# Residual layer norm: the DRAM rows of a partition in blocks of 24, 24 and 16 instead of 64, with 27 transfers in place of 24

## The chip, the cores and the metric

One core of one Trainium2 chip. The time is device microseconds (us) of one execution, the median of several. A comparison is given as a ratio with a 95% interval: the mean time of one kernel's fast runs over that of the other's of the same rounds on the same chip, so it is not quite the ratio of the medians that are quoted beside it.

## The reference

```
z = x + residual                      # x, residual: 16 x 1024 x 512, float32
mean, var = z.mean(-1), z.var(-1)
out = gamma * (z - mean) / sqrt(var + eps) + beta
```

16,384 rows of 512 elements: 33.55 MB each of x, residual and out.

## The kernel before

There are 128 rows for each of the 128 partitions. GpSimd (POOL) adds x and residual, ScalarE (ACT) takes mean, sum of squares and root, VectorE (DVE) normalises, in turns of 4 rows. x and the result share a ring of 64 rows (zbuf), the residual and the sum a ring of 32 (rbuf). All large transfers go through the sync engine's queue in the order of a plan; `x0+16` is a load of rows 0 to 15 of x, `r` of the residual, `o` a store.

```
BLOCK = 64
PLAN = """
x0+16 r0+8 r8+24 x16+20 x36+28 r32+16 o0+16 o16+8
r48+16 x64+24 r64+16 o24+24 r80+16 x88+16 r96+12 o48+16
x104+8 r108+8 x112+16 r116+12 o64+16 o80+24 o104+16 o120+8
"""
    def dram(t, lo, n):                # which DRAM rows are row lo.. of each partition
        b0 = lo - lo % BLOCK
        v = t[P * b0 : P * (b0 + BLOCK), :].rearrange("(p j) d -> p j d", p=P)
        return v[:, lo - b0 : lo - b0 + n, :].rearrange("p a b -> p (a b)")
... (cut)
    for kind, lo, n in moves:          # the sync engine, in the order of the plan
        if kind == "x":                # the ring's old rows must be stored
            while gone < len(stores) and stores[gone][0] < lo + n - Z_ROWS:
                nc.sync.wait_ge(so[gone], 16)
                gone += 1
            move(part(zbuf, Z_ROWS, lo, n), dram(xf, lo, n), sx[...])
        elif kind == "r":              # the ring's old rows must be used up by DVE
            ... (cut)
        else:                          # the rows must be finished
            ... (cut)
```

With a block of 64, the 64 rows of a partition lie together in DRAM, and the next partition starts 64 x 2 KB = 128 KB further on. This distance is called the pitch below. Each transfer becomes one packet per partition, so 8 for each of the 16 DMA engines (the 3456 packets of the queue are 24 x (128 + 16); the 16 are of 4 bytes).

Of the kernel before, what the change touches and what calls it, by code (L numbers as in the profile page):

```python
# [8 lines left out]
FP32 = mybir.dt.float32  # L9
# [1 line left out]
ALU = mybir.AluOpType  # L11


BLOCK = 64
Z_ROWS = 64
R_ROWS = 32


PLAN = """
x0+16 r0+8 r8+24 x16+20 x36+28 r32+16 o0+16 o16+8  # L20
r48+16 x64+24 r64+16 o24+24 r80+16 x88+16 r96+12 o48+16
x104+8 r108+8 x112+16 r116+12 o64+16 o80+24 o104+16 o120+8
"""


ADDS = [4] * 32


TURN = 4
R_TURNS = R_ROWS // TURN  # L30
Z_TURNS = Z_ROWS // TURN


EARLY = 2
# [3 lines left out]
def kernel(  # L38
# [9 lines left out]
    nc = tc.nc  # L48
    P = nc.NUM_PARTITIONS
# [3 lines left out]
    N, D = xf.shape  # L53
    inv_d = 1.0 / float(D)
    total = N // P


    tc.close()
    tc.compile()  # L59
# [1 line left out]
    moves = []  # L61
    for word in PLAN.split():
        kind, (lo, n) = word[0], map(int, word[1:].split("+"))
        assert lo // BLOCK == (lo + n - 1) // BLOCK
        moves.append((kind, lo, n))

    def of_kind(kind):
# [3 lines left out]

    def dram(t, lo, n):

        b0 = lo - lo % BLOCK
        v = t[P * b0 : P * (b0 + BLOCK), :].rearrange("(p j) d -> p j d", p=P)
        return v[:, lo - b0 : lo - b0 + n, :].rearrange("p a b -> p (a b)")

    zbuf = nc.alloc_sbuf_tensor("zbuf", [P, Z_ROWS * D], FP32)
# [4 lines left out]
    nm, ssq, std, rstd = (  # L83
        nc.alloc_sbuf_tensor(name, [P, R_ROWS], FP32) for name in ("nm", "ssq", "std", "rstd")
    )
    gamma_p = nc.alloc_psum_tensor("gamma_p", [P, D], FP32)
    beta_p = nc.alloc_psum_tensor("beta_p", [P, D], FP32)
    junk_m = [nc.alloc_psum_tensor(f"junk_m{i}", [P, D], FP32) for i in range(TURN)]
    junk_s = [nc.alloc_psum_tensor(f"junk_s{i}", [P, D], FP32) for i in range(6 - TURN)]
    junk_s += [  # L90
        nc.alloc_sbuf_tensor(f"junk_s{i}", [P, D], FP32) for i in range(6 - TURN, TURN)
    ]

    sems = []
# [1 line left out]
    def sem(name):  # L96
        s = nc.alloc_semaphore(name)
        sems.append(s)
        return s
# [5 lines left out]
    s_const = sem("const")  # L105
    s_pe = sem("pe")
    s_sum, s_mean, s_ssq, s_std = (
        [sem(f"{name}{j}") for j in range(R_TURNS)] for name in ("sum", "mean", "ssq", "std")
    )
    s_rstd = [sem(f"rstd{j}") for j in range(Z_TURNS)]  # L110
    s_out = sem("out")
    so = [sem(f"so{c}") for c in range(len(stores))]
    nums = [s.num for s in sems]
# [2 lines left out]
    def part(buf, size, lo, n):  # L116
        assert lo % size + n <= size
        return buf[:, (lo % size) * D : (lo % size + n) * D]
# [16 lines left out]
    seen = 0  # L135
    first = []

    def move(out, in_, s):
        i = nc.sync.dma_start(out=out, in_=in_).then_inc(s, 16)  # L139
        if len(first) < EARLY:  # L140
            first.append(i.ins)

    gone = 0
    for kind, lo, n in moves:
        if kind == "x":
# [3 lines that stand above are left out]
            move(part(zbuf, Z_ROWS, lo, n), dram(xf, lo, n), sx[loads_x.index((lo, n))])  # L149
        elif kind == "r":  # L150
            if lo + n > R_ROWS:
                last = (lo + n - R_ROWS) // TURN - 1
                nc.sync.wait_ge(s_rstd[last % Z_TURNS], last // Z_TURNS + 1)
            move(part(rbuf, R_ROWS, lo, n), dram(rf, lo, n), sr[loads_r.index((lo, n))])
        else:
            if lo + n > seen:
                nc.sync.wait_ge(s_out, lo + n)
                seen = lo + n
            move(dram(of, lo, n), part(zbuf, Z_ROWS, lo, n), so[stores.index((lo, n))])


# [5 lines left out]


    landed = {"x": 0, "r": 0}
    lo = 0  # L170
    for n in ADDS:
        for key, loads, s in (("x", loads_x, sx), ("r", loads_r, sr)):
            while landed[key] < len(loads) and loads[landed[key]][0] < lo + n:
                nc.gpsimd.wait_ge(s[landed[key]], 16)
                landed[key] += 1
        z = part(rbuf, R_ROWS, lo, n)
        nc.gpsimd.tensor_tensor(  # L177
            out=z, in0=part(zbuf, Z_ROWS, lo, n), in1=z, op=ALU.add
        ).then_inc(s_sum[lo // TURN % R_TURNS], 1)
        lo += n  # L180
    assert lo == total



# [1 line left out]
    def column(t, lo, n=1):  # L186
        return t[:, lo % R_ROWS : lo % R_ROWS + n]
# [5 lines left out]
    with act.Fori(0, total // R_ROWS) as lap:  # L193
        hints.append(act.mark_branch_hint_location())
        due = act.snap(lap + 1)
        for j in range(R_TURNS):
            rows = range(j * TURN, (j + 1) * TURN)
            act.wait_ge(s_sum[j], due)
            for k, r in enumerate(rows):
                i = act.activation(  # L200
                    out=junk_m[k][:, :],
                    in_=part(rbuf, R_ROWS, r, 1),
                    func=ACT.Identity,
                    scale=-inv_d,
                    accum_out=column(nm, r),
                )
            i.then_inc(s_mean[j], 1)
            act.wait_ge(s_mean[j], due)
            for k, r in enumerate(rows):
                i = act.activation(  # L210
                    out=junk_s[k][:, :],
                    in_=part(rbuf, R_ROWS, r, 1),
                    func=ACT.Square,
                    bias=column(nm, r),
                    accum_out=column(ssq, r),
                )
            i.then_inc(s_ssq[j], 1)
            act.wait_ge(s_ssq[j], due)
            act.activation(  # L219
                out=column(std, rows[0], TURN),  # L220
                in_=column(ssq, rows[0], TURN),
                func=ACT.Sqrt,
                bias=eps_t[:, 0:1],
                scale=inv_d,
            ).then_inc(s_std[j], 1)


    dve = nc.vector
    dve.wait_ge(s_pe, 2)
    with dve.Fori(0, total // Z_ROWS) as lap:  # L230
        hints.append(dve.mark_branch_hint_location())
        due = [dve.snap(lap * 2 + 1), dve.snap(lap * 2 + 2)]
        turn = dve.snap(lap + 1)
        for j in range(Z_TURNS):
            rows = range(j * TURN, (j + 1) * TURN)
            dve.wait_ge(s_std[j % R_TURNS], due[j // R_TURNS])
            for r in rows:
                dve.scalar_tensor_tensor(  # L238
                    out=part(zbuf, Z_ROWS, r, 1),
                    in0=part(rbuf, R_ROWS, r, 1),  # L240
                    scalar=column(nm, r),
                    in1=gamma_p[:, :],
                    op0=ALU.add,
                    op1=ALU.mult,
                )
            dve.reciprocal(  # L246
                out=column(rstd, rows[0], TURN), in_=column(std, rows[0], TURN)
            ).then_inc(s_rstd[j], 1)
            dve.wait_ge(s_rstd[j], turn)
            for r in rows:  # L250
                z = part(zbuf, Z_ROWS, r, 1)
                i = dve.scalar_tensor_tensor(  # L252
                    out=z,
                    in0=z,
                    scalar=column(rstd, r),
                    in1=beta_p[:, :],
                    op0=ALU.mult,
                    op1=ALU.add,
                )
            i.then_inc(s_out, TURN)  # L260


    loops = [b for b in nc.main_func.blocks if b.name.endswith("_loop")]
# [48 lines left out]
```

## Time and profile before

| | before |
|---|---|
| time, median | 238.22 us at first; 238.04 with all 6 runs beside the changed kernel |
| span of the profile | 236.9 us |
| the data queue's share of 16 engines | 99.3% |
| busiest compute engine | ACT, 78% |
| bytes moved | 100.67 MB |

The page, the stretches and the sync engine's waits are shown and read in the prediction. One thing that the prediction lacks can be had from the packet records: a transfer ends on each engine with a packet of 4 bytes (384 of them for the 24 transfers, 9 ns each), so sorting these in groups of 16 tells when each engine was done with it. (The records don't name the engine; the groups rest on the order in time.) A "round" is one packet on each of the 16 engines.

```
kernel before          first engine   mean    last engine   last - mean
end of x0+16              11.27       11.54      11.76          0.23
end of r32+16             70.37       70.57      70.92          0.35
end of the last store    235.31      235.81     236.43          0.62
```

### The profile page before, as it was taken

The page shows a single profiled execution, that of the slowest core. Times are in us where ns is not written, and L with a number is a line of the kernel's source. Part 1 is how long each engine was busy: PE and PEld are TensorE (multiplying, and loading weights), DVE is VectorE, ACT ScalarE, POOL GpSimd, SP SyncE. Part 2 cuts the span into 40 slices and gives each one's busy share as a digit, 9 for nine tenths or more (in the row PEclk, how much of TensorE's full clock was granted, in tenths as well). Part 3 has the DMA queues.
Part 4 walks back from the last instruction along what each step waited for, and adds up shares of the span by engine and source line. Part 5 has one row for each costly group of instructions (what it writes and reads, how often), then busy time and mean ns, then how long its engine had stood idle before and what let it go on. Part 6 is the DMA issues. An engine that isn't in the chain of part 4 may idle for free.

```text
span 236.9 us, 985 instructions
## 1 busy us (share of the span) xinstructions
PE 4.1 (2%) x4; PEld 1.0 (0%) x4; DVE 177.2 (75%) x290; ACT 184.1 (78%) x545; POOL 144.1 (61%) x36
## 2 busy tenths in 40 slices
PE   0600000000000000000000000000000000000000
PEld 0100000000000000000000000000000000000000
DVE  0000395898999299979997999889999999979900
ACT  2003968999992999799989999899999999799100
POOL 0019468699409990899179936999939375970000
DMA  9999999979999999999999899999999999999997
GB/s 354 399 443 473 456 408 415 508 329 465 443 354 443 393 465 423 490 398 398 443 407 506 382 426 431 422 431 441 409 423 451 425 436 429 479 407 431 437 396 329
DMA packets 3461, 100.67 MB, mean 425 GB/s; under 512 B 387, under 2 KB 387, under 8 KB 389
## 3 DMA queue, kind: packets, MB, share of 16 engines
q1 hardware_dynamic: 3456, 100.66, 99.3%
q10 hardware_dynamic: 4, 0.00, 0.0%
q14 instruction: 1, 0.00, 0.0%
HBM read 67.11 MB, written 33.55 MB: 425 GB/s over the span
## 4 chain that ended last, share of the span: by engine, by line
DMA 44%; ACT 36%; POOL 8%; DVE 6%; issue 1%; SPq 0%; DVEq 0%
DMA rbuf<-in_residual_dram 26%; ACT junk_s L210 19%; DMA zbuf<-in_x_dram 17%; ACT junk_m L200 16%; POOL rbuf L177 8%; DVE zbuf L238 5%; ACT std L219 2%; DVE zbuf L252 1%; DVE rstd L246 0%; SPq L139 0%; DVEq L230 0%
## 5 line engine op out<-in xcount | busy, mean ns | idle before, releaser
L177 POOL TENSOR_TENSOR rbuf<-zbuf,rbuf 128x2048 f32<-128x2048 f32 x32 | 143.9, 4528 | 67.3 <-DMA rbuf<-in_residual_dram 54.2
L238 DVE SCALAR_TENSOR_TENSOR zbuf<-rbuf,nm,gamma_p 128x512 f32<-128x512 f32 x128 | 87.1, 743 | 45.3 <-ACT std L219 45.3
L200 ACT ACTIVATE junk_m<-rbuf 128x512 f32<-128x512 f32 x128 | 74.3, 581 | 31.1 <-POOL rbuf L177 30.9
L210 ACT ACTIVATE junk_s<-rbuf,nm 128x512 f32<-128x512 f32 x128 | 88.9, 694 | 1.0
L252 DVE SCALAR_TENSOR_TENSOR zbuf<-zbuf,rstd,beta_p 128x512 f32<-128x512 f32 x128 | 87.1, 744 | 1.1
L210 ACT ACTIVATION_READ_ACCUMULATOR junk_s<-rbuf,nm 128x1 f32 x128 | 23.9, 187 | 0.0
L200 ACT ACTIVATION_READ_ACCUMULATOR junk_m<-rbuf 128x1 f32 x128 | 23.9, 186 | 0.0
L219 ACT ACTIVATE std<-ssq,eps_t 128x4 f32<-128x4 f32 x32 | 9.5, 297 | 1.0
L246 DVE RECIPROCAL rstd<-std 128x4 f32<-128x4 f32 x32 | 5.5, 171 | 0.0
L191 ACT ACT_TABLE_LOAD x1 | 1.3, 1283 | 2.7 <-PEq L59 2.7
L130 PE MATMUL gamma_p<-gb_row,ones 1*128 1x512 f32 x2 | 2.0, 1122 | 7.3 <-DMA gb_row<-in_gamma_dram 7.3
L130 PE MATMUL beta_p<-gb_row,ones 1*128 1x512 f32 x2 | 2.1, 1136 | 0.4 <-DMA gb_row<-in_beta_dram 0.4
L125 DVE MEMSET ones<- 1x128 f32 x1 | 0.2, 165 | 2.0 <-PEq L59 2.0
L130 PEld LDWEIGHTS gamma_p<-gb_row,ones 1*128 1x128 f32 x2 | 0.5, 308 | 7.3 <-issue 7.3
L130 PEld LDWEIGHTS beta_p<-gb_row,ones 1*128 1x128 f32 x2 | 0.5, 304 | 2.0 <-DMA gb_row<-in_beta_dram 2.0
L293 POOL MEMSET const-float32-0.0<- 128x1 f32 x1 | 0.1, 98 | 0.2 <-issue 0.2
L293 POOL MEMSET const-bfloat16-1.0<- 128x1 bf16 x1 | 0.1, 101 | 0.0
L293 POOL MEMSET const-uint8-127<- 128x1 uint8 x1 | 0.1, 101 | 0.0
L293 POOL MEMSET const-float32-1.0<- 128x1 f32 x1 | 0.1, 98 | 0.0
L126 DVE MEMSET eps_t<- 128x1 f32 x1 | 0.1, 59 | 0.0
## 6 DMA issues: line engine op xcount, KB each, us to landing
rbuf<-in_residual_dram SPq DMA_DIRECT2D x4, 4096.0 KB, 19.4
out_dram<-zbuf SPq DMA_DIRECT2D x4, 4096.0 KB, 26.8
zbuf<-in_x_dram SPq DMA_DIRECT2D x3, 4096.0 KB, 19.3
out_dram<-zbuf SPq DMA_DIRECT2D x2, 6144.0 KB, 31.5
zbuf<-in_x_dram SPq DMA_DIRECT2D x1, 7168.0 KB, 57.8
rbuf<-in_residual_dram SPq DMA_DIRECT2D x1, 6144.0 KB, 29.6
zbuf<-in_x_dram SPq DMA_DIRECT2D x1, 6144.0 KB, 23.7
rbuf<-in_residual_dram SPq DMA_DIRECT2D x2, 3072.0 KB, 19.8
```

What stands on the lines that cost most here:

```text
L125: nc.vector.memset(ones[:, :], 1.0).then_inc(s_const, 1)
L126: nc.vector.memset(eps_t[:, :], float(eps)).then_inc(s_const, 1)
L130: nc.tensor.matmul(dest[:, :], ones[:, :], gb_row[:, k * D : (k + 1) * D], start=True, stop=True).then_inc(s_pe, 1)
L177: nc.gpsimd.tensor_tensor(out=z, in0=part(zbuf, Z_ROWS, lo, n), in1=z, op=ALU.add).then_inc(s_sum[lo // TURN % R_TURNS], 1)
L191: act.preload_act_table_set("sqrt_and_others")
L200: i = act.activation(out=junk_m[k][:, :], in_=part(rbuf, R_ROWS, r, 1), func=ACT.Identity, scale=-inv_d, accum_out=column(nm, r),)
L210: i = act.activation(out=junk_s[k][:, :], in_=part(rbuf, R_ROWS, r, 1), func=ACT.Square, bias=column(nm, r), accum_out=column(ssq, r),)
L219: act.activation(out=column(std, rows[0], TURN), in_=column(ssq, rows[0], TURN), func=ACT.Sqrt, bias=eps_t[:, 0:1], scale=inv_d,).then_inc ...
L238: dve.scalar_tensor_tensor(out=part(zbuf, Z_ROWS, r, 1), in0=part(rbuf, R_ROWS, r, 1), scalar=column(nm, r), in1=gamma_p[:, :], op0=ALU.ad ...
L246: dve.reciprocal(out=column(rstd, rows[0], TURN), in_=column(std, rows[0], TURN)).then_inc(s_rstd[j], 1)
L252: i = dve.scalar_tensor_tensor(out=z, in0=z, scalar=column(rstd, r), in1=beta_p[:, :], op0=ALU.mult, op1=ALU.add,)
L293: nc = _bacc.Bacc("TRN2", target_bir_lowering=False, num_devices=1)
```

## The change

Every transfer's rows are to lie in one DRAM block, so a load of 24 rows becomes one contiguous piece of 6 MB, and the pitch falls to 48 KB (32 KB in the blocks of 16). The plan is recut to fit; the opening load grows from 16 to 24 rows and the last store shrinks from 8 to 4. The rest of the diff generalises the arithmetic of rows and turns; the turns stay 32 of 4 rows.

```
-BLOCK = 64
+BLOCKS = [24, 24, 16]
 PLAN = """
-x0+16 r0+8 r8+24 x16+20 x36+28 r32+16 o0+16 o16+8
-r48+16 x64+24 r64+16 o24+24 r80+16 x88+16 r96+12 o48+16
-x104+8 r108+8 x112+16 r116+12 o64+16 o80+24 o104+16 o120+8
+x0+24 r0+8 r8+16 x24+24 r24+8 x48+16 r32+16 o0+16 o16+8
+r48+16 x64+24 r64+16 o24+24 r80+8 r88+8 x88+24 r96+8 o48+16
+r104+8 r112+8 x112+16 r120+8 o64+24 o88+24 o112+8 o120+4 o124+4
 """
-ADDS = [4] * 32
-TURN = 4
+TURNS = [4]
... (cut)
-        b0 = lo - lo % BLOCK
-        v = t[P * b0 : P * (b0 + BLOCK), :].rearrange("(p j) d -> p j d", p=P)
+        k = spot(blocks, lo)
+        b0, b1 = blocks[k], blocks[k + 1]
+        v = t[P * b0 : P * b1, :].rearrange("(p j) d -> p j d", p=P)
... (cut: the same turns counted from a list of marks)
```

More of the change, by code (lines that the diff above doesn't have):

```diff
@@ L19 @@
 PLAN = """
-x0+16 r0+8 r8+24 x16+20 x36+28 r32+16 o0+16 o16+8
-r48+16 x64+24 r64+16 o24+24 r80+16 x88+16 r96+12 o48+16
-x104+8 r108+8 x112+16 r116+12 o64+16 o80+24 o104+16 o120+8
-"""
-ADDS = [4] * 32
-TURN = 4
-R_TURNS = R_ROWS // TURN
-Z_TURNS = Z_ROWS // TURN
+x0+24 r0+8 r8+16 x24+24 r24+8 x48+16 r32+16 o0+16 o16+8
+r48+16 x64+24 r64+16 o24+24 r80+8 r88+8 x88+24 r96+8 o48+16
+r104+8 r112+8 x112+16 r120+8 o64+24 o88+24 o112+8 o120+4 o124+4
+"""
+TURNS = [4]
 EARLY = 2
@@ L55, with edges, spot @@
     total = N // P
+    def edges(sizes, end):
+        found, k = [0], 0
+        while found[-1] < end:
+            found.append(found[-1] + sizes[k % len(sizes)])
+            k += 1
+        assert found[-1] == end
+        return found
+    def spot(marks, row):
+        return max(k for k, m in enumerate(marks) if m <= row)
+    blocks = edges(BLOCKS, total)
+    marks = edges(TURNS, total)
+    most = max(TURNS)
+    r_turns, z_turns = spot(marks, R_ROWS), spot(marks, Z_ROWS)
+    assert marks[r_turns] == R_ROWS and marks[z_turns] == Z_ROWS
+    assert z_turns == 2 * r_turns
     tc.close()
@@ L63 @@
         kind, (lo, n) = word[0], map(int, word[1:].split("+"))
-        assert lo // BLOCK == (lo + n - 1) // BLOCK
+        assert spot(blocks, lo) == spot(blocks, lo + n - 1)
         moves.append((kind, lo, n))
@@ L87 @@
     beta_p = nc.alloc_psum_tensor("beta_p", [P, D], FP32)
-    junk_m = [nc.alloc_psum_tensor(f"junk_m{i}", [P, D], FP32) for i in range(TURN)]
-    junk_s = [nc.alloc_psum_tensor(f"junk_s{i}", [P, D], FP32) for i in range(6 - TURN)]
+    junk_m = [nc.alloc_psum_tensor(f"junk_m{i}", [P, D], FP32) for i in range(most)]
+    junk_s = [nc.alloc_psum_tensor(f"junk_s{i}", [P, D], FP32) for i in range(6 - most)]
     junk_s += [
-        nc.alloc_sbuf_tensor(f"junk_s{i}", [P, D], FP32) for i in range(6 - TURN, TURN)
+        nc.alloc_sbuf_tensor(f"junk_s{i}", [P, D], FP32) for i in range(6 - most, most)
     ]
@@ L107 @@
     s_sum, s_mean, s_ssq, s_std = (
-        [sem(f"{name}{j}") for j in range(R_TURNS)] for name in ("sum", "mean", "ssq", "std")
+        [sem(f"{name}{j}") for j in range(r_turns)] for name in ("sum", "mean", "ssq", "std")
     )
-    s_rstd = [sem(f"rstd{j}") for j in range(Z_TURNS)]
+    s_rstd = [sem(f"rstd{j}") for j in range(z_turns)]
     s_out = sem("out")
@@ L151 @@
             if lo + n > R_ROWS:
-                last = (lo + n - R_ROWS) // TURN - 1
-                nc.sync.wait_ge(s_rstd[last % Z_TURNS], last // Z_TURNS + 1)
+                last = spot(marks, lo + n - R_ROWS - 1)
+                nc.sync.wait_ge(s_rstd[last % z_turns], last // z_turns + 1)
             move(part(rbuf, R_ROWS, lo, n), dram(rf, lo, n), sr[loads_r.index((lo, n))])
@@ L156 @@
             if lo + n > seen:
-                nc.sync.wait_ge(s_out, lo + n)
-                seen = lo + n
+                seen = next(m for m in marks if m >= lo + n)
+                nc.sync.wait_ge(s_out, seen)
             move(dram(of, lo, n), part(zbuf, Z_ROWS, lo, n), so[stores.index((lo, n))])
@@ L169 @@
     landed = {"x": 0, "r": 0}
-    lo = 0
-    for n in ADDS:
+    for k in range(len(marks) - 1):
+        lo, n = marks[k], marks[k + 1] - marks[k]
         for key, loads, s in (("x", loads_x, sx), ("r", loads_r, sr)):
@@ L178 @@
             out=z, in0=part(zbuf, Z_ROWS, lo, n), in1=z, op=ALU.add
-        ).then_inc(s_sum[lo // TURN % R_TURNS], 1)
-        lo += n
-    assert lo == total
+        ).then_inc(s_sum[k % r_turns], 1)
     def column(t, lo, n=1):
@@ L195 @@
         due = act.snap(lap + 1)
-        for j in range(R_TURNS):
-            rows = range(j * TURN, (j + 1) * TURN)
+        for j in range(r_turns):
+            rows = range(marks[j], marks[j + 1])
             act.wait_ge(s_sum[j], due)
@@ L219 @@
             act.activation(
-                out=column(std, rows[0], TURN),
-                in_=column(ssq, rows[0], TURN),
+                out=column(std, rows[0], len(rows)),
+                in_=column(ssq, rows[0], len(rows)),
                 func=ACT.Sqrt,
@@ L233 @@
         turn = dve.snap(lap + 1)
-        for j in range(Z_TURNS):
-            rows = range(j * TURN, (j + 1) * TURN)
-            dve.wait_ge(s_std[j % R_TURNS], due[j // R_TURNS])
+        for j in range(z_turns):
+            rows = range(marks[j], marks[j + 1])
+            dve.wait_ge(s_std[j % r_turns], due[j // r_turns])
             for r in rows:
@@ L246 @@
             dve.reciprocal(
-                out=column(rstd, rows[0], TURN), in_=column(std, rows[0], TURN)
+                out=column(rstd, rows[0], len(rows)), in_=column(std, rows[0], len(rows))
             ).then_inc(s_rstd[j], 1)
@@ L259 @@
                 )
-            i.then_inc(s_out, TURN)
+            i.then_inc(s_out, len(rows))
     loops = [b for b in nc.main_func.blocks if b.name.endswith("_loop")]
```

## The prediction

> **What bounds the kernel now.** I started with the page of the kernel before: the busy shares (part 1), the slices (part 2), the queues (part 3) and the chain that ended last (part 4).
>
> ```profile
> span 236.9 us, 985 instructions
> PE 4.1 (2%) x4; PEld 1.0 (0%) x4; DVE 177.2 (75%) x290; ACT 184.1 (78%) x545; POOL 144.1 (61%) x36
> DMA  9999999979999999999999899999999999999997
> GB/s 354 399 443 473 456 408 415 508 329 465 443 354 443 393 465 423 490 398 398 443 407 506 382 426 431 422 431 441 409 423 451 425 436 429 479 407 431 437 396 329
> q1 hardware_dynamic: 3456, 100.66, 99.3%
> DMA 44%; ACT 36%; POOL 8%; DVE 6%; issue 1%; SPq 0%; DVEq 0%
> ```
>
> No compute engine is over 78% busy, but the one queue that carries the data keeps the 16 DMA engines at work for 99.3% of the span, and the slices show a 9 nearly everywhere. The last line misleads on a first look: it gives ACT 36% of the chain, because it follows the semaphore waits from the last compute back. Those waits bind only if the DMA engines ever run dry, and 99.3% says they don't. The GB/s of a slice jump from 329 to 508 because the bytes of a whole packet fall in one slice; only their mean, 425, carries meaning.
>
> Next I took the stretches view, to see where the DMA is below full rate (columns: stretch, its length, busy time of PE, PE load, DVE, ACT, POOL with counts, PE clock, DMA share, GB/s):
>
> ```profile
> 15.00:60.00 45.00, 0.00 (x0) 0.00 (x0) 27.75 (x46) 34.52 (x103) 34.22 (x8) 1.00 1.01 436
> 60.00:70.00 10.00, 0.00 (x0) 0.00 (x0) 9.76 (x17) 9.90 (x30) 1.71 (x1) 1.00 1.00 393
> 196.00:237.00 41.00, 0.00 (x0) 0.00 (x0) 27.03 (x45) 22.28 (x67) 13.49 (x3) 1.00 0.96 415
> ```
>
> In 60 to 70 us the engines are fully busy and yet move less: packets take longer there. So I read the single packet records of the trace (start, duration, size), which the views only sum up. Every transfer is 128 packets, one per partition, 8 on each engine, each of (rows x 2 KB). Medians:
>
> ```
> packet KB   16     24     32     40     48     56
> us          0.611  0.915  1.213  1.514  1.815  2.116
> ```
>
> Each 8 KB more costs 0.301 us, that is 37.6 ns per KB, and 0.009 us is left over per packet. Ten in a hundred at most are slower. From this the whole span can be built, per engine: 384 rows (128 of x, of residual and of out) x 8 packets x 2 KB x 37.6 ns = 231.0 us of pure bytes; 24 transfers x (8 x 9.5 ns, and 9 ns for the semaphore packet) = 2.0 us; packets slower than the line summed over all engines and divided by 16 = 2.2 us. Sum 235.2; the first data packet starts at 1.03 us and the last ends at 236.42, the span at 236.9, and the timed run has 1.3 us more (238.22). **The bound is the byte rate of the DMA engines**, 231 of 238 us.
>
> Where do the 2.2 us of slow packets sit? 0.55 in the first round of the kernel (all 16 packets of it, 1.1 to 1.7 times the normal time), 0.89 between 65 and 70 us, in one round of r32+16 (up to 1.79 times), shortly before the first stores; the rest in pieces of at most 0.15 us, mostly at changes between loads and stores (at about 118, 158 and 196 us).
>
> **How far from starving is it?** The sync engine issues in order and waits for free buffers. Its waits:
>
> ```profile
> SPq L139 <- DVE rstd L246: 116.6, 7, 47.3
> SPq L139 <- DVE zbuf L252: 65.8, 6, 24.4
> SPq L139 <- DMA out_dram<-zbuf: 21.5, 2, 13.2
> ```
>
> They are long, but harmless as long as the queue holds older transfers. Setting each issue in the timeline against the end of the transfer queued ahead of it (from the packet records) gives the backlog:
>
> ```profile
> 50.63 0.33 SPq L139 DMA_DIRECT2D rbuf<-in_residual_dram  x1
> 74.25 0.34 SPq L139 DMA_DIRECT2D rbuf<-in_residual_dram  x1
> 86.47 0.34 SPq L139 DMA_DIRECT2D zbuf<-in_x_dram  x1
> 126.19 0.33 SPq L139 DMA_DIRECT2D rbuf<-in_residual_dram  x1
> 175.31 50.69 SPq L139 DMA_DIRECT2D out_dram<-zbuf  x4
> ```
>
> r32+16 is issued at 50.63 while x36+28 runs to 60.21: 9.6 us of backlog. r48+16: 11.2 us; x64+24: 8.7; r80+16: 8.0. The last of the four stores of the last line, o120+8, is issued at 225.66 (175.31 is where the group begins) with o104+16 running to 231.56: 5.9 us, the smallest of all.
>
> [...] 37.6 ns per KB x 16 engines is 435.7 GB/s. [...] the page above shows 425. [...] This is what the change is after: its pitch between partitions falls from 128 KB to 48 KB (32 KB in the last block), and transfers of 24 rows become contiguous. But the trace before, with its pitch of 128 KB, shows nearly all packets on the ceiling, so there is little here to cure.
>
> **The change part by part.**
> 1. *Blocks of 24, 24, 16 in place of 64.* Only DRAM addresses change. SBUF side, bytes and packet sizes per row stay. It can touch only the slow packets, 2.2 us. The 0.55 at the opening is a cold start and I leave it. Of the other 1.66 us some could go if address conflicts make it; that they sit near changes of direction, which the new plan has as often (seven: r32 to o0, o16 to r48, r64 to o24, o24 to r80, x/r96 to o48, o48 to r104, r120 to o64), says much would stay. I take a bit over a third: -0.65 us.
> 2. *27 transfers in place of 24.* 3 x (8 x 9.5 + 9) ns = +0.26 us on each engine, on the bound itself.
> 3. *The opening.* x0+24, r0+8 puts 32 rows ahead of the first add in place of 24: 8 x 0.61 = 4.9 us later, about 22.0 in place of 17.15. Rows 8 to 15 still land after 48 rows, at about 31.1. ACT works 5.75 us per turn of 4 rows without a break from about 26.6, ends row 15 at about 49.7 and DVE frees it 2.8 later, about 52.5 in place of 50.6. So r32+16 goes out 1.9 us later, with 7.7 us of backlog in place of 9.6. r48+16 follows after four more turns (23 us), at about 75.6 in place of 74.25: backlog about 9.8. Hidden.
> 4. *The middle.* 64 rows of x and 32 of residual, then r32+16, o0+16, o16+8, r48+16, x64+24, r64+16, o24+24 are of the same size and order as before from here on. x88+24 waits for the landing of o24+24, as x88+16 did; 16 rows of residual (9.8 us) lie behind that store in both, so the backlog is the 9.1 us of before, less a few tenths. Hidden.
> 5. *The tail.* 320 rows lie ahead of the end of the last load in both plans, so it lands at about 198. Then POOL 4.5, two to four turns of ACT and 5.6 of DVE: the last rows are ready at about 225 in both. The stores behind it are 64 rows, 39 us, so the queue ends at about 236 either way; cutting the last store to 4 rows raises the backlog at the last issue (a wait for rows 120 to 127 becomes one for 124 to 127), and nothing can be gained from a backlog that is never used up.
> 6. The code for turns gives the same 32 turns of 4; compute instructions stay.
>
> Sum: 238.22 + 0.26 - 0.65 = 237.83, say **237.8 us**.
>
> **Rivals.** (a) *Address conflicts cause all slow packets but the opening*: -1.66 + 0.26, 236.8 us. For it: the slow round at 65 us hits all 16 engines at once. Against: the seven other rounds of that transfer, of the same pitch, run at the ceiling. (b) *Direction changes cause them*: nothing gained, 238.5. (c) *The new pitch conflicts*[...]. One such slow round per direction change, 0.9 us x 3, would give about 241; a loss of 5% of the rate 250. [...] (d) *The queue starves*: by the 4.9 us of the later start if the backlog were gone; but it is 5.9 at the least before and about 7 here, so it would need two such delays at once. (e) *Faster by over 2%*, under 233.5: excluded by the sum, 231.0 of bytes + 2.3 of packets + 1.0 opening + 1.8 end = 236.1 with no slow packet at all.
>
> **Range and chances.** (a) to (b) spans 236.8 to 238.5; with 0.3 at the low end and 0.7 above for some of (c), 236.5 to 239.2. Faster 0.01, within 2% 0.96, slower 0.03.
>
> **What would show it.** The queue at 99% or more again, 27 x 144 = 3888 packets on it; the medians 1.213 and 1.815 us for 32 and 48 KB unchanged; the first POOL add at about 22; r32+16 issued at about 52.5 while the loads ahead run to 60; slow packets of 1 to 2.2 us, the round at 65 gone or not. A DMA share under 97% in a middle stretch would mean starving, longer median packets a conflict of addresses: either would make me wrong.

(That the old pitch cost anything was not shown. The sum came to 238.22 + 0.26 - 0.65 = 237.83 us. The -0.65 was my estimate, a bit over a third of the 1.66 us of slow packets outside the first round, 2.2 less 0.55. "The ceiling" is the line through the packet medians, 37.6 ns per KB. "Cold start" is a name for the slow first round, 1.1 to 1.7 times the normal time; no trace shows what makes it slow.)

## More of the kernel before

"Before" was run anew beside each group of experiments, with medians of 238.28 us (e), 238.26 (f) and 238.29 (g and h). The e and f runs were made on one chip, the g runs on a second, the h runs on a third.

## The result, and the profile after

239.06 us, the median of 6 runs (238.80 to 240.17), against 238.04 (237.90 to 238.25): ratio 1.0049, interval 1.0029 to 1.0070. The kernel is slower by about half a per cent, and its runs scatter by 1.4 us where those before scatter by 0.35. Within 2% it is the same; the interval still says that something costs about a microsecond.

The page of the changed kernel (the span, the slices, the data queue):

```profile
span 238.2 us, 993 instructions
DMA  9989999999999999999999999999999999999895
GB/s 363 413 388 470 424 451 421 399 435 440 440 369 429 424 451 473 396 446 435 451 429 396 418 443 495 404 388 454 413 426 459 435 437 465 398 413 479 385 409 241
q1 hardware_dynamic: 3888, 100.67, 98.8%
```

The middle is as full as before. What is new stands at the right edge: the last slices read 8, 9, 5 where they read 9, 9, 7, the last moves 241 GB/s in place of 329, and the share is 98.8% in place of 99.3%. The stretches view of the last microseconds (the last two columns are DMA share and GB/s), first of the kernel before:

```profile
235.00:236.00 1.00, 0.00 (x0) 0.00 (x0) 0.00 (x0) 0.00 (x0) 0.00 (x0) 1.00 0.50 213
236.00:237.00 1.00, 0.00 (x0) 0.00 (x0) 0.00 (x0) 0.00 (x0) 0.00 (x0) 1.00 0.00 0
237.00:238.00 1.00, 0.00 (x0) 0.00 (x0) 0.00 (x0) 0.00 (x0) 0.00 (x0) 1.00 0.00 0
```

then of the changed one:

```profile
235.00:236.00 1.00, 0.00 (x0) 0.00 (x0) 0.00 (x0) 0.00 (x0) 0.00 (x0) 1.00 0.40 164
236.00:237.00 1.00, 0.00 (x0) 0.00 (x0) 0.00 (x0) 0.00 (x0) 0.00 (x0) 1.00 0.21 90
237.00:238.00 1.00, 0.00 (x0) 0.00 (x0) 0.00 (x0) 0.00 (x0) 0.00 (x0) 1.00 0.04 16
```

A share of 0.21 of 16 engines is three or four engines still at work while the others have nothing left. (A packet is counted where it starts.) The ends of transfers say the same:

```
changed kernel         first engine   mean    last engine   last - mean
end of x0+24              16.22       16.67      17.54          0.86
end of r32+16             70.14       70.82      72.23          1.42
end of the last store    235.04      235.81     237.70          1.89
```

The mean end is 235.81 us in both kernels. The whole difference of these two runs, 239.55 - 238.28 = 1.27 us, is the lag of the last engine behind that mean: 1.89 - 0.62 = 1.27. (The profiled run of the changed kernel was 0.5 us over its median. The mean end lies between 235.37 and 235.84 us in all kernels below, so that these two agree so closely is chance.) Of the 1.27, 0.63 is there when the first load is done (0.86 - 0.23), 0.44 more comes up to the end of r32+16, the rest later. Four engines are over 0.4 us behind the mean at the end of all 27 transfers. They are the same four: almost every packet starts within a few ns of the end of an earlier one, so the records can be strung into 16 chains of 243 packets, and the four chains that end the first load last (17.27 to 17.54 us) are the four that end the kernel last (236.66 to 237.70; no other after 235.83). In the first round of packets, which start between 1.02 and 1.76 us, of 48 KB and 1.815 us when served at full rate, four took 2.86 to 3.67 us and the others 1.86 to 2.72.

So the question is what makes the engines uneven in the opening: the larger first packet, the layout in DRAM, or the number of transfers.

### The profile page after: what moved, and what is told of

It is laid out like the page before. It is cut to its first block, busy times and chain, and to the rows that moved or that the text cites. A ratio compares the mean times of both kernels' runs of the same rounds, so it can differ in the third digit from the quotient of the medians.

```text
span 238.2 us, 993 instructions
## 1 busy us (share of the span) xinstructions
PE 4.1 (2%) x4; PEld 1.0 (0%) x4; DVE 177.2 (74%) x290; ACT 183.7 (77%) x545; POOL 144.1 (60%) x36
## 3 DMA queue, kind: packets, MB, share of 16 engines
q1 hardware_dynamic: 3888, 100.67, 98.8%
## 4 chain that ended last, share of the span: by engine, by line
ACT 43%; DMA 40%; POOL 6%; DVE 6%; issue 1%; SPq 0%; ACTq 0%; DVEq 0%; POOLq 0%
ACT junk_s L222 22%; ACT junk_m L212 19%; DMA rbuf<-in_residual_dram 17%; DMA out_dram<-zbuf 13%; DMA zbuf<-in_x_dram 10%; POOL rbuf L191 6%; DVE zbuf L250 3%; ACT std L231 2%; DVE zbuf L264 2%; SPq L153 0%; DVE rstd L258 0%; ACTq L205 0%; DVEq L242 0%; ACTq L210 0%; ACTq L206 0%
```

## The experiments

All results are correct. "Lag" is the distance of the last engine behind the mean, that of the one profiled run of each. Each time is to be set against the "before" of its own group, as the ratio does.

| run | pitch of the first load | first packet | transfers | lag after first x load | lag at the end | median us | ratio to before, interval |
|---|---|---|---|---|---|---|---|
| before | 128 KB | 32 KB | 24 | 0.23 | 0.62 | 238.04 | |
| changed | 48 KB | 48 KB | 27 | 0.86 | 1.89 | 239.06 | 1.0049, 1.0029 to 1.0070 |
| h3_again (changed) | 48 KB | 48 KB | 27 | 0.90 | 1.78 | 239.10 | 1.0034, 1.0020 to 1.0047 |
| e1_block64 | 128 KB | 48 KB | 27 | 0.18 | 0.73 | 238.25 | 1.0004, 0.9990 to 1.0017 |
| e2_open16 | 48 KB | 32 KB | 28 | 0.47 | 0.87 | 238.95 | 1.0032, 1.0019 to 1.0046 |
| e3_open4 | 48 KB | 8 KB | 28 | 0.26 | 0.90 | 238.12 | 0.9992, 0.9978 to 1.0006 |
| e4_before_open24 | 128 KB | 48 KB | 24 | 0.22 | 1.06 | 238.16 | 0.9994, 0.9980 to 1.0008 |
| f1_b24_40 | 48 KB | 48 KB | 27 | 0.92 | 1.60 | 238.95 | 1.0041, 1.0027 to 1.0054 |
| f2_b64_then24 | 128 KB | 48 KB | 27 | 0.20 | 0.92 | 238.03 | 0.9991, 0.9978 to 1.0005 |
| f3_b48_16 | 96 KB | 48 KB | 27 | 0.74 | 1.70 | 238.94 | 1.0010, 0.9990 to 1.0030 |
| f4_64_small | 128 KB | 8 KB | 29 | 0.27 | 0.83 | 238.34 | 1.0007, 0.9994 to 1.0019 |
| g1_b16_48 | 32 KB | 32 KB | 29 | 0.29 | 1.03 | 238.26 | 1.0002, 0.9989 to 1.0015 |
| g2_early_store | 128 KB | 48 KB | 28 | 0.40 | 0.62 | 238.40 | 1.0007, 0.9993 to 1.0022 |
| g3_warm | 128 KB | 48 KB | 27 | 0.29 | 0.99 | 238.54 | 1.0010, 0.9997 to 1.0023 |
| g4_r_first | 48 KB | 16 KB | 27 | 0.62 | 1.41 | 238.43 | 1.0011, 0.9994 to 1.0029 |
| h1_b32 | 64 KB | 48 KB | 29 | 0.42 | 0.68 | 238.20 | 1.0005, 0.9992 to 1.0018 |
| h2_b28 | 56 KB | 48 KB | 30 | 0.18 | 0.78 | 238.23 | 0.9999, 0.9986 to 1.0012 |
| h4_64_open4 | 128 KB | 8 KB | 28 | 0.43 | 0.68 | 238.39 | 1.0008, 0.9995 to 1.0021 |

(g4_r_first: the lag is that after r0+8, its first load. e3, f4 and h4: after x0+4.)

**Layout, size or number (e1 to e4).** First the layout alone was undone:

```
-BLOCKS = [24, 24, 16]      # e1_block64
+BLOCKS = [64]
```

> The changed kernel with its 27 transfers, but rows in DRAM blocks of 64 as before. In the profile of the changed kernel the mean over the 16 DMA engines of the end of the last transfer is the same as before (235.81 us in both), but the slowest engine ends 1.89 us after that mean in place of 0.62. Theory 1 (the first packet, 48 KB in place of 32, is served at a cold and uneven rate and the unlucky engine stays behind to the end): layout is neutral, about 239.0 us, spread after x0+24 about 1.3 us. Theory 2 (the pitch of 48 KB makes the service uneven): about 238.3, spread after x0+24 about 0.5. Theory 3 (the three more transfers cost more than their 0.26 us): 239.0 too, but with even engines.

238.25 us, as before, and the lag after x0+24 is 0.18 us. The edge of the page closes again:

```profile
DMA  9989999999999999999999899999999999999997
GB/s 399 399 385 440 432 470 398 421 465 443 443 354 443 398 465 443 465 398 398 443 440 481 357 429 462 432 407 445 443 404 459 426 404 476 408 465 448 407 386 322
q1 hardware_dynamic: 3888, 100.67, 99.3%
```

Same plan, same 3888 packets, 99.3% again and a last slice of 7. My theory 1, that the larger first packet alone does it, falls here; theory 2, the pitch, holds. Its counterpart puts the large opening into the kernel before:

```
-x0+16 r0+8 r8+24 x16+20 x36+28 ...      # e4_before_open24, blocks of 64
+x0+24 r0+8 r8+24 x24+12 x36+28 ...
```

> The kernel before, blocks of 64 and 24 transfers, with only its opening changed: 24 rows of x first (x0+24 r0+8 r8+24 x24+12 x36+28). Theory 1: the spread after x0 rises to about 1.3 us and the time by about 0.6, to 238.65. Theories 2 and 3: 238.05, as before.

238.16 us, lag 0.22: the large opening costs nothing at a pitch of 128 KB. Then the first packet was made smaller with the new layout kept:

```
-x0+24 r0+8 ...
+x0+16 x16+8 r0+8 ...      # e2_open16
+x0+4 x4+20 r0+8 ...       # e3_open4
```

> The changed kernel, layout and all, with the first load of 24 rows cut into 16 and 8 (28 transfers), so the first packets are of 32 KB as before. Theory 1: spread after the opening back to 0.5 us, about 238.5 us. Theory 2: no better than the changed kernel, 239.0 or 239.1. Theory 3: 239.15.

> The changed kernel with the first load cut into 4 and 20 rows, so the first packets are of 8 KB. If the cold loss is in proportion to the first packet (mean factor 1.46 at 32 KB and 1.47 at 48 KB), it falls from 0.86 us to about 0.15 and the spread to about 0.2 us: 237.9 to 238.2. If it lasts a fixed time of 2 to 3 us whatever the packets are, the loss moves into the packets that follow and little is won: 238.8. Theories 2 and 3: 239.1.

e2 stays slow at 238.95. Its profile is of its fastest run (238.22), so the lag of 0.47 is a low one; even so four packets of its first round took 1.8 to 2.05 times the full-rate time. The transfer x0+16 is not contiguous in a block of 24, so contiguity isn't what hurts. e3 is back at 238.12 with a lag of 0.26, though all its other rows lie at the new pitch. Neither fixed theory has it quite: in these runs the loss needs the pitch of 48 KB *and* large packets in the first round.

**Which block (f1, f2).** If only the opening matters, only the first block should. The list of blocks is repeated until all 128 rows are covered, so in f1 rows 64 to 87 have the pitch of 48 KB too, and not 80 KB as the expectation says of all later rows; f2 has that pitch in rows 64 to 111 only.

```
-BLOCKS = [24, 24, 16]
+BLOCKS = [24, 40]             # f1_b24_40
+BLOCKS = [64, 24, 24, 16]     # f2_b64_then24
```

> The changed kernel with blocks of 24 and 40 rows: the opening still reads with a pitch of 48 KB between partitions, all later rows with 80 KB. Theory 2a (the pitch of 48 KB hurts in the opening, where all 16 engines start at once, and the loss stays on the unlucky engines): about 239.0, three or four engines over 0.5 us behind after x0+24. Theory 2b (the loss comes from the later blocks, or from their number): about 238.4.

> The changed kernel with one block of 64 rows and then 24, 24, 16: the opening has the old pitch of 128 KB, the second half of the rows the new one. Theory 2a: about 238.3, as with blocks of 64 all through. Theory 2b: 238.7 to 239.0.

The first is slow (238.95, lag 0.92), the second isn't (238.03, lag 0.20) although half of its rows, stores too, lie in blocks of 24 and 16. Since f2 clears the blocks from row 64 on, the place of the loss is the first block. The stretches view shows the edge open in f1_b24_40:

```profile
236.00:237.00 1.00, 0.00 (x0) 0.00 (x0) 0.00 (x0) 0.00 (x0) 0.00 (x0) 1.00 0.12 49
```

and all but closed in f2_b64_then24:

```profile
236.00:237.00 1.00, 0.00 (x0) 0.00 (x0) 0.00 (x0) 0.00 (x0) 0.00 (x0) 1.00 0.02 8
```

**Which pitch (f3, g1, h1, h2).** The same 24-row first load at 96, 64 and 56 KB, and a 16-row one at 32 KB; where a transfer would cross a block, it is cut in two.

```
+BLOCKS = [48, 16]         # f3_b48_16: 96 KB
+BLOCKS = [16, 48, 64]     # g1_b16_48: 32 KB, opening x0+16 x16+8 r0+8 r8+8 r16+8
+BLOCKS = [32, 32, 64]     # h1_b32: 64 KB, cuts at row 32
+BLOCKS = [28, 36, 64]     # h2_b28: 56 KB, cuts at row 28
```

> The changed kernel with blocks of 48 and 16 rows: the opening reads with a pitch of 96 KB. If every pitch that is not a power of two is uneven in the opening, about 239.0; if only the pitch of 48 KB is, or only contiguous transfers are (x0+24 is no longer contiguous in DRAM), about 238.3.

> The plan of the changed kernel with blocks of 16, 48 and 64 rows and the opening x0+16 x16+8 r0+8 r8+8 r16+8 (29 transfers): the first load has the packets of 32 KB of the run with the opening of 16 rows, but reads with a pitch of 32 KB, contiguous as well. Theory 2c (the pitch must be a power of two for the engines to be served evenly at the start): no engine over 0.4 us behind the mean after x0, 238.1 to 238.4. Theory 2d (small pitches are uneven, whatever they are): 238.9 or more.

> The plan of the changed kernel in blocks of 32, 32 and 64 rows, the transfers of x and out at rows 24 to 47 cut at row 32 (29 transfers). The first load is x0+24 with packets of 48 KB as in the changed kernel, at a pitch of 64 KB. If pitches that are a power of two serve the engines evenly (32 KB and 128 KB did), 238.1 to 238.4 and no engine over 0.4 us behind the mean after x0+24; if small pitches with packets of 48 KB don't, 239.0.

> The same with blocks of 28, 36 and 64 rows, cut at row 28 (30 transfers): packets of 48 KB at a pitch of 56 KB. If pitches that are no power of two serve the engines unevenly at the start (48 and 96 KB did), an engine ends x0+24 0.7 to 0.9 us behind the mean and the time is 238.8 to 239.1; if 48 and 96 KB are special, 238.3.

32, 56, 64 and 128 KB are even enough (238.2 to 238.3; in h1 one engine lags by 0.42, just over the 0.4 that I had allowed); so it isn't small pitches, and, with 56 KB, not pitches that are no power of two. 96 KB is in between: four of its six runs took 238.93 to 239.05, two 237.74 and 237.99, and in the profiled one a single engine was over 0.4 us late where the changed kernel has four, or two in its repeat; its ratio doesn't separate it from before. What is particular to 48 KB stays open: no view shows which DRAM addresses conflict, or that it is a conflict of addresses at all. Two rivals are untested: where in DRAM the tensors begin, which no run varied, and the chip, for 32 KB, since the changed kernel wasn't run beside the g runs.

**How the lag depends on the first packet (g4).** The two first loads swapped, nothing else:

```
-x0+24 r0+8 ...
+r0+8 x0+24 ...      # g4_r_first
```

> The changed kernel, blocks of 24, 24 and 16 and 27 transfers, with only the first two loads swapped (r0+8 ahead of x0+24), so the first packets are of 16 KB in place of 48. If the unlucky engines are served at about half the rate of the others for their first packet, their lag shrinks in proportion, from about 0.9 us behind the mean to about 0.3, and the time to 238.3 or less. If the lag were a fixed time, or came with x0+24 wherever it stands, 239.0.

A miss for both: 238.43 us, but from 237.94 to 239.37, and a lag of 0.62. It is less than with packets of 48 KB and more than a third of it.

**The second slow round (f4, g2, g3).** Every kernel here has one round that is slow on all engines, shortly before the first store (0.89 us, the mean of the engines, in the kernel before, where the 16 packets that start from 67.0 to 67.5 us take 1.49 to 1.79 times the normal time, and 0.79 us in the changed one). The late engines lose most in it: the lag went from 0.87 to 1.42 in the changed kernel, from 0.92 to 1.53 in its repeat, 0.92 to 1.56 in f1 and 0.75 to 1.46 in f3, but by no more than 0.16 in any kernel whose lag was under 0.45 (e2 and g4, in between, went from 0.47 to 0.51 and from 0.63 to 0.87; in h4 the lag even fell, from 0.40 to 0.22). Three runs asked what makes it, all with blocks of 64.

```
-x0+24 r0+8 ... r32+16 o0+16 ...
+x0+4 x4+20 r0+8 ... r32+12 r44+4 o0+16 ...              # f4_64_small
+x0+24 r0+8 ... r24+8 o0+4 x48+16 r32+16 o4+12 ...       # g2_early_store
+    nc.scalar.dma_start(out=dram(of, 0, 1)[:, 0:128], in_=warm[:, :]) ...    # g3_warm: dummy store
```

> The plan of the changed kernel in blocks of 64, with small packets where the two slow rounds are: x0+4 x4+20 at the start and r32+12 r44+4 ahead of the first store (29 transfers). If the slow rounds cost a share of their packet (1.5 to 1.8 times), both losses shrink to a quarter, together 1.0 us less: 237.2. If they cost a fixed time of 0.5 to 0.8 us each, it stays at 238.1 to 238.3.

> The plan of the changed kernel in blocks of 64, with 4 rows stored early (o0+4 ahead of x48+16, o4+12 where o0+16 was). All kernels so far have a slow round two packets ahead of their first store, 0.5 to 0.8 us over all engines, at 65 to 70 us. If the first store makes it, it moves to the packets of r24+8, at about 48 to 52 us, and the place at 67 us is clean. If something at that time of the run makes it, it stays. The time stays at about 238.3 either way.

> The plan of the changed kernel in blocks of 64, with a dummy store of 512 bytes per partition to the output's first rows at the start, overwritten later by the real store, which waits for it. If the slow round ahead of the first store is the price of the first write to the output, and is paid beside the slow opening instead, about 0.5 us is won: 237.7. If it comes with every first large store, 238.3.

With the early store the slow round moved to 47.5 to 51.5 us (0.94 us, the mean of the engines, there) and the place at 65 to 70 was clean; the stretches view has it in the GB/s (last column). First g2_early_store:

```profile
45.00:55.00 10.00, 0.00 (x0) 0.00 (x0) 9.75 (x17) 9.90 (x30) 7.70 (x3) 1.00 1.03 400
60.00:75.00 15.00, 0.00 (x0) 0.00 (x0) 14.40 (x24) 12.60 (x39) 2.19 (x2) 1.00 0.98 424
```

then e1_block64, the same plan without the early store:

```profile
45.00:55.00 10.00, 0.00 (x0) 0.00 (x0) 9.76 (x17) 9.90 (x30) 8.50 (x3) 1.00 0.99 426
60.00:75.00 15.00, 0.00 (x0) 0.00 (x0) 14.40 (x24) 12.42 (x38) 4.00 (x2) 1.00 1.00 411
```

The early store lowers the first stretch from 426 to 400 and raises the second from 411 to 424. So the round goes with the first store, and comes already while the load packets ahead of it run. In f4, with packets of 8 KB in both slow places, the loss stayed before the store (0.88 us, where e1 has 0.75), and in the opening it fell only to 0.44 from the 0.74 of e1 with its packets of 48 KB: it doesn't shrink with the packet. In h4, with packets of 8 KB too, the opening cost 0.9 to 1.0 us. The dummy store of 64 KB didn't take away the slow round before the first large store (0.73 us, time 238.54).

**The repeat and the best of both (h3, h4).**

> The changed kernel again, unaltered, on this chip beside the others: its single profile so far was of a run 0.5 us over its median. The late engines after x0+24 are to be there again (0.7 to 1.0 us behind the mean), the mean end of the engines at 235.4 to 235.8, and the time at 238.8 to 239.2. If the lag after x0+24 is missing at that time, the theory falls.

> Blocks of 64, the plan of the changed kernel, first load cut into 4 and 20 rows: the best of what was found put together. At the most 0.3 us under the kernel before: 238.0; the lags at the end come from other places (the tail of stores) and stay.

The repeat agrees: lag 0.90 after x0+24, 1.78 at the end, mean end 235.67, 239.10 us. Two engines are over 0.4 us behind after x0+24 there, and four at the end; so the number of late engines changes from run to run, and that one is late doesn't. Blocks of 64 with the small opening gave 238.39, no better than before and a miss of the 238.0 that I expected. No kernel tried beats the kernel before: the lowest, f2, has the interval 0.9978 to 1.0005.

## Why the prediction was wrong where it was

- **The bound** was right: the packet medians of 32 and 48 KB are 1.213 and 1.815 us again, and 3888 packets ran. (The queue's share, 98.8%, just missed the 99% that I had named: the open edge at the end.)
- **The step that failed is part 1**, "I take a bit over a third: -0.65 us". It counted slow packets "summed over all engines and divided by 16". By that measure the changed kernel gained 0.2 us (2.0 us of slow packets in place of 2.2), but e1, the same plan in blocks of 64, has 1.9 to 2.0 as well: the new layout itself gained nothing. And the kernel ends with its *last* engine, and the term for that is missing in my sum. It measured +1.27 us in the profile. The layout makes it: undone, 238.25; with the pitch of 48 KB in rows 0 to 23 and 64 to 87 alone, 238.95.
- **Rival (c)** came nearest, with the new pitch as the cause, but with the wrong size and place: I expected it at every change of direction, 3 x 0.9 us (my own part 1 counts seven such changes, not three), and let it into the range alone, not into the sum. It sits in the opening, and that it is a conflict of addresses isn't shown. The sign that I had set for it, longer median packets, was blind to it: the medians didn't move.
- **The opening (part 3)** I checked only for starvation, and that part was sound. The first add came at 22.87 (22.0 said), r32+16 was issued at 53.35 (52.5) and r48+16 at 76.32 (75.6): each later by 0.7 to 0.9 us, about the lag of the slowest engine: the add waits for r0+8, which the mean engine ended at 21.54 and the last at 22.40. "The 0.55 at the opening is a cold start and I leave it" was the wrong place to stop looking: I had its factors, 1.1 to 1.7, and didn't ask what becomes of their spread.
- **The three transfers (part 2, +0.26)** can't be seen: e1, with 27, has 0.9990 to 1.0017, which holds 0 and +0.26. h2, with 30, has 0.9986 to 1.0012; six transfers at that rate are +0.51 us, or 1.0021, outside. Its profile has 1.8 us of slow packets in place of 2.2, which offsets most of it.
- **The tail (part 5)** came with a wrong time and the right backlog: the last rows were ready at 227.9 in place of 225, but the last store, issued at 227.95, still had 7.0 us until the last engine was done with the transfer ahead (234.97), and 5.4 until the mean engine was. Nothing starved, so it cost nothing.
- **Direction and range.** I said 237.8, a gain of 0.2%, and got 239.06, a loss of 0.5%; "within 2%" was right, and the range up to 239.2 just holds the median.

What stays open: why 48 KB is uneven and 56 KB isn't, and why engines that were late already lost more at the first store.

## What to carry to other kernels

Where the DMA engines are the bound (their queue was busy for 98.8 to 99.3% of the span here), look at when each of them ends and not only at their mean share: the engines that were served badly in the opening here were still late 220 us later (the last by 0.86 us after the first load and by 1.89 after the last store), since each had its own share of 243 packets and no pause to catch up in, and the kernel waited for them. Read the last slices and the end of the first load for that, before and after a change of layout or opening. If a layout is needed that serves the first packets unevenly, try a small first load: packets of 8 KB took most of the harm away here (238.12 us, ratio to before 0.9992, in place of 239.06 and 1.0049).

A contiguous load isn't served evenly by that alone: the first load of 24 rows at the pitch of 48 KB, one piece of 6 MB, came with a loss of 0.8 to 1.0 us (239.10 against 238.29 in the repeat, 239.06 against 238.04 at first), with four of 16 first packets at 2.86 to 3.67 us where the others took 1.86 to 2.72.

Two places of these kernels cost more than the line of the packet medians: the first packets, 0.44 us (f4, packets of 8 KB) to 0.9 to 1.0 (h4, 8 KB too), the mean of the engines, and the loads just ahead of the first store, 0.73 us (g3) to 0.94 (g2), which moved with that store (from about 67 to 71 us in e1 to 47.5 to 51.5 in g2).

The last store of the changed kernel, 1 MB behind other transfers, moved the mean end of the engines by 2.47 us (233.34 to 235.81), the time of its 8 packets per engine at 0.309 us each.
